# Two blocks or four at a time: the order of high and low matmuls in 128-feature tiles

## The chip, the cores and the metric

The kernel runs on one core of a Trainium2 chip. The metric is the device time of one execution in microseconds (us). The core has five engines that are meant here by these names: PE (TensorE, the matmuls), PEld (its weight loads), DVE (VectorE), ACT (ScalarE), POOL (GpSimd); SP (SyncE) issues the DMA transfers.

## What is computed

The reference is a two-layer decoder trunk over 256 tokens of width 2048. Cut to what matters for the matmuls:

```
u = rms_norm(x) @ w_in                      # 2048 x 2048, each layer
token_out = pooling mixer (layer 0) or differential attention (layer 1)
x = x + concat(token_out, mem_out) @ w_out  # 2048 x 2048, each layer
h = rms_norm(x)
z = relu(h @ w_ff1)                         # 2048 x 8192, each layer
x = x + (z * z) @ w_ff2                     # 8192 x 2048, each layer
```

There are also the key and value projections of a memory of 256 tokens and, between the layers, the shared keys and values. All inputs and outputs are fp32.

## The kernel before

**Two parts for each number.** Every fp32 weight and every fp32 activation is split into a high part (rounded to the matmul's fp32r format) and a low part (the rest). A product is the sum of three matmuls: high by high, high weight by low activation, low weight by high activation.

**The weights' way.** Weights are laid out in blocks of 128x128 in the order in which they are used, and eight blocks make one row in memory. The class `Feed` (lines 106 to 250) loads rows by SP, and splits them ahead of use: `_split` (lines 152 to 160) lets ACT cast 128x512 to the high ring (line 157) and lets DVE subtract to make the low ring (line 158). Four blocks that lie side by side in the rings, 512 columns, are called a quad here. Each ring has six slots of 512 columns. `fill`, called when a quad is begun, splits up to three jobs ahead of the one in use, if slots are free. ACT's cast into a slot waits for PE's last read of the high part there; DVE's subtraction waits for the cast and for PE's last read of the low part there.

**A tile of 128 features** is made by `a_part` (lines 377 to 397). A result has 128 features by 256 tokens. The weight block is the stationary operand, and the activations `xs[:, k, :]` are the moving one, with 256 columns of high parts and 256 of low parts next to each other. So the high block takes one matmul of 512 columns ("wide", line 391) into a whole bank of 512 columns, and the low block one matmul of 256 columns ("narrow", line 393) into the bank's second half, by the high activations alone. Both halves are added when the bank is emptied. `a_part` takes two blocks at a time: two wide matmuls, then two narrow ones, and again. A tile with 2048 inputs takes 16 blocks, four quads, and so eight such rounds.

```
            for c, k, hi, lo in two:
                nc.tensor.matmul(ps, hi, xs[:, k, :], start=first and c == 0, stop=False)
            for c, k, hi, lo in two:
                nc.tensor.matmul(
                    ps[:, T : 2 * T], lo, xs[:, k, 0:T], start=False,
                    stop=last and c == len(ks) - 1,
                )
```

Its callers: `group_u` (the pooling mixer's inputs, 12 tiles), `out_tiles` (w_out, 32 tiles), `up_tile` and `down_tile` of `ffn` (w_ff1 and half of w_ff2, 191 tiles). Together these are 235 tiles and 3760 blocks, a wide and a narrow matmul for each.

**Other matmuls from the rings.** `wide_step` (lines 412 to 421) makes the weights the moving operand: only wide matmuls, lines 417 to 419. `product` (lines 741 to 748) does the same for the other half of w_ff2. `c_tile` (lines 400 to 409) and `group_w` (lines 1020 to 1022) use narrow matmuls only, three for each block.

**In the feed-forward part** the bank of an up or down tile, `x_bank`, is a single one. After each tile ACT copies it out (`evict`, line 672), and `product` runs 6 or 9 wide matmuls on other banks before the next tile begins. In the last stretch of a feed-forward part, single `product` jobs stand between the quads of a tile.

**What sets the order.** The lines of the program give the order in which work is asked for; `at` and `tick` put small steps (attention, activation functions, splits) at the ends of quads. A scheduler then sets each engine's own queue; its order of ACT's and DVE's instructions follows the readiness that it expects, so that a change in PE's order can move them too.

Of the kernel before, what the change touches and what calls it, by code (L numbers as in the profile page):

```python
# [19 lines left out]
T = 256  # L20
NK = 16
# [241 lines left out]
def program(ctx, tc, plan, dry, xT, memT, par, lam, cst, wst, yT):  # L263
    nc = tc.nc
# [7 lines left out]
    feed = Feed(nc, wst, wp, tp, plan, dry)  # L272
# [10 lines left out]
    def tick():  # L283
        now[0] += 1
        for fn in pend.pop(now[0], []):
            fn()
# [9 lines left out]
    def mmt(name):  # L296
        return pp.tile([P, 512], F32, tag="mm", bufs=3, name=name)
# [79 lines left out]
    def a_part(ps, w, l, n, ks, xs, first=True, last=True, between=None):  # L377


        ks = list(ks)  # L380
        i = 0
        while i < len(ks):
            if between:
                between(i)
            two = []
            for k in ks[i : i + 2 - feed.pos % 2]:
                two.append((i, k % NK, *feed.block((w, l, k, n, 1))))
                feed.used()
                i += 1
            for c, k, hi, lo in two:  # L390
                nc.tensor.matmul(ps, hi, xs[:, k, :], start=first and c == 0, stop=False)  # L391
            for c, k, hi, lo in two:
                nc.tensor.matmul(  # L393
                    ps[:, T : 2 * T], lo, xs[:, k, 0:T], start=False,
                    stop=last and c == len(ks) - 1,
                )
            if feed.pos % 4 == 0:
                tick()

# [248 lines left out]
    def ffn(l, xs, tags, done):  # L648
# [57 lines left out]
        def up_tile(q, i, ps):  # L706
            a_part(ps, "w_ff1", l, q * NK + i, range(NK), xs)
            if not r:
                r.append(rstd_from("x"))
            y = evict(ps)  # L710

            def first():
                nc.vector.tensor_add(y[:, 0:T], y[:, 0:T], y[:, T : 2 * T])
                stt(y[:, 0:T], y[:, 0:T], 0.0, r[0], ALU.max, ALU.mult)

            at(1, first)
            at(3, lambda: nc.scalar.activation(stage[i % 8], y[:, 0:T], AF.Square))  # L717
            if q == 0 or i > 0:
                convert(i, 3)

        def down_tile(q, n, ps, between=None):
            end = l == 1 and q == 3 and n == 7
            if end:
                c_tile(ps, "w_ff2", l, n, range(q * NK, q * NK + NK), z)
                nc.vector.tensor_add(resid[:, n, :], resid[:, n, :], ps[:, 0:T])
                done(n)
                return
            a_part(ps, "w_ff2", l, n, range(q * NK, q * NK + NK), z, between=between)
            x = evict(ps)

            def add():
                nc.vector.tensor_add(resid[:, n, :], resid[:, n, :], x[:, 0:T])
                nc.vector.tensor_add(resid[:, n, :], resid[:, n, :], x[:, T : 2 * T])
                if q == 3:
                    done(n)

            at(1, add)
# [152 lines left out]
    xs = sp.tile([P, NK, 512], F32R, tag="S2", name="xs0")  # L890
# [67 lines left out]
    ps = [mmt("mq0"), pp.tile([P, 512], F32, tag="o", bufs=1, name="mq0")]  # L958
# [22 lines left out]
    def group_u(g):  # L981
        up = ups[g % 2]
        for c in range(3):
            ps = mmt("u")
            a_part(ps, "w_in", 0, 3 * g + c, range(NK), xs)
            low = vt("u_c")
            nc.scalar.copy(low, ps[:, T : 2 * T])
            nc.vector.tensor_add(low, ps[:, 0:T], low)
            nc.vector.tensor_mul(up[:, c, 16:], low, x_r[0])
# [106 lines left out]
    def pair_of_banks(c, name):  # L1096
        if c % 2:
            return [pp.tile([P, 512], F32, tag="s", bufs=2, name=name) for _ in range(2)]
        return [mmt(name) for _ in range(2)]
# [3 lines left out]
    for c in range(3):  # L1103
        ps = pair_of_banks(c, "k1")
# [10 lines left out]
    for c in range(3):  # L1115
        ps = pair_of_banks(c + 1, "v1")
# [9 lines left out]
    ps = pair_of_banks(0, "mk1")  # L1126
# [4 lines left out]
    ps = pair_of_banks(1, "mv1")  # L1131
# [132 lines left out]
    for c in range(3):  # L1264
        ps = pair_of_banks(0, "q1")
# [14 lines left out]
    for h in range(4):  # L1280
        ps = mmt("mq1")
# [95 lines left out]
```

## Time and profile before

| what | value |
|---|---|
| median of 3 runs | 2045.59 us (2045.58 to 2047.15) |
| the profiled execution | 2044.93 us |
| its span, first to last instruction | 2043.1 us |
| granted TensorE clock | 1.00 |
| wide matmuls of line 391 | 3760, mean recorded length 395 to 401 ns |
| narrow matmuls of line 393 | 3760, mean recorded length 278 to 281 ns |
| weight loads | 11060, one for each matmul, most of them 188 ns |
| DMA, mean over the span | 191 GB/s |

Recorded lengths of matmuls overlap: a matmul begins before the one ahead of it has ended. What a matmul costs PE is therefore read from the distance between two starts, which the timeline gives, and not from its length. "Idle before" is the time that an engine stood still ahead of an instruction, with the one that ended it.

### The profile page before, as it was taken

What the parts mean: (1) busy time and instruction counts of PE and PEld (TensorE: products, weight loads), DVE (VectorE), ACT (ScalarE), POOL (GpSimd) and SP (SyncE); (2) the same over time, 40 slices, a digit from 0 to 9 for tenths busy, and PEclk for the clock granted to TensorE, in tenths of its full rate; (3) what the DMA queues carried; (4) which work ended last, traced back from release to release, by engine and by line L of the source; (5) the groups of instructions that cost most, each with busy time, mean ns of one, the idle gap of its engine ahead of it and who ended that gap; (6) DMA issues with size and microseconds to landing.
All of it is one profiled execution on the core that took longest, in us unless ns stands there. A gap on an engine that the chain in (4) does not pass through costs nothing.

```text
span 2043.1 us, 32257 instructions
## 1 busy us (share of the span) xinstructions
PE 2037.2 (100%) x11060; PEld 1755.3 (86%) x11060; DVE 1716.2 (84%) x3215; ACT 1349.8 (66%) x2505; POOL 51.9 (3%) x67
## 2 busy tenths in 40 slices
PE   9999999999999999999999999999999999999999
PEld 8888888888888888888888888888888888888888
DVE  8888889889879978999766687889879978988997
ACT  7765566666666756768665697566657666666764
POOL 0001200000000000000000000310000000000000
PEclk9999999999999999999999999999999999999999
DMA  9556556555555555655565543656555555565564
GB/s 314 178 181 190 188 174 206 197 196 197 186 201 202 189 207 191 207 169 182 194 228 186 170 140 103 196 166 207 196 196 205 186 196 196 186 210 195 196 209 135
DMA packets 110470, 390.75 MB, mean 191 GB/s; under 512 B 12256, under 2 KB 14944, under 8 KB 110304
## 3 DMA queue, kind: packets, MB, share of 16 engines
q1 hardware_dynamic: 110160, 388.59, 57.1%
q8 instruction: 86, 1.41, 0.3%
q14 instruction: 80, 0.66, 0.1%
q10 hardware_dynamic: 144, 0.10, 0.0%
HBM read 386.54 MB, written 2.10 MB: 190 GB/s over the span
## 4 chain that ended last, share of the span: by engine, by line
PE 99%; ACT 1%; DVE 1%; issue 0%
PE x_bank L391 33%; PE x_bank L393 16%; PE wo L391 6%; PE p L746 5%; PE p L747 5%; PE p L748 5%; PE wo L393 3%; PE u L391 2%; PE ff L391 2%; PE u L393 1%; PE k L417 1%; PE k L419 1%; PE v L417 1%; PE k L418 1%; PE v L419 1%; PE v L418 1%
## 5 line engine op out<-in xcount | busy, mean ns | idle before, releaser
L157 ACT CAST hi_ring<-raw 128x512 fp32r<-128x512 f32 x1193 | 736.7, 620 | 529.5 <-PE x_bank L391 308.0
L158 DVE TENSOR_TENSOR lo_ring<-raw,hi_ring 128x512 fp32r<-128x512 f32 x1193 | 817.2, 695 | 206.7 <-ACT hi_ring L157 165.5
L391 PE MATMUL x_bank<-fx,hi_ring 128*128 128x512 f32 x1920 | 602.1, 395 | 0.0
L393 PEld LDWEIGHTS x_bank<-fx,lo_ring 128*128 128x128 f32 x1920 | 361.0, 188 | 83.6
L393 PE MATMUL x_bank<-fx,lo_ring 128*128 128x256 f32 x1920 | 377.4, 278 | 0.0
L391 PEld LDWEIGHTS x_bank<-fx,hi_ring 128*128 128x128 f32 x1920 | 301.4, 189 | 9.3
L391 PE MATMUL x_bank<-z,hi_ring 128*128 128x512 f32 x960 | 301.1, 395 | 0.0
L158 DVE TENSOR_TENSOR lo_ring<-slab,hi_ring 128x1024 fp32r<-128x1024 f32 x188 | 230.1, 1224 | 54.3 <-ACT hi_ring L157 53.6
L157 ACT CAST hi_ring<-slab 128x1024 fp32r<-128x1024 f32 x188 | 196.9, 1047 | 73.1 <-PE x_bank L391 36.2
L393 PEld LDWEIGHTS x_bank<-z,lo_ring 128*128 128x128 f32 x960 | 180.5, 188 | 41.7
L393 PE MATMUL x_bank<-z,lo_ring 128*128 128x256 f32 x960 | 188.8, 278 | 0.0
L391 PE MATMUL wo<-cat,hi_ring 128*128 128x512 f32 x512 | 162.5, 398 | 0.5 <-DVE resid L639 0.5
L391 PEld LDWEIGHTS x_bank<-z,hi_ring 128*128 128x128 f32 x960 | 151.9, 189 | 6.5 <-ACT room L672 0.4
L393 PEld LDWEIGHTS wo<-cat,lo_ring 128*128 128x128 f32 x512 | 95.9, 188 | 21.7
L672 ACT COPY room<-x_bank 128x512 f32<-128x512 f32 x180 | 104.9, 583 | 2.0 <-PE x_bank L393 2.0
L393 PE MATMUL wo<-cat,lo_ring 128*128 128x256 f32 x512 | 101.4, 279 | 0.0
L746 PE MATMUL p<-hi_ring,sit 128*128 128x512 f32 x256 | 100.5, 393 | 0.0
L747 PE MATMUL p<-hi_ring,sit 128*128 128x512 f32 x256 | 100.2, 391 | 0.0
L748 PE MATMUL p<-lo_ring,sit 128*128 128x512 f32 x256 | 99.7, 389 | 0.0
L391 PEld LDWEIGHTS wo<-cat,hi_ring 128*128 128x128 f32 x512 | 79.1, 189 | 2.2 <-PE wo L393 0.9
L717 ACT ACTIVATE room<-room 128x256 f32<-128x256 f32 x128 | 53.2, 416 | 39.1 <-DVE room L300 39.1
L746 PE MATMUL p<-hi_ring,z 128*128 128x512 f32 x192 | 75.2, 392 | 0.0
(313 smaller groups left out, 3102.3 us busy)
## 6 DMA issues: line engine op xcount, KB each, us to landing
raw<-in_w SPq DMA_DIRECT2D x595, 512.0 KB, 4.0
slab<-in_w SPq DMA_DIRECT2D x124, 512.0 KB, 3.3
resid<-in_x SPq DMA_DIRECT2D x8, 256.0 KB, 5.9
room<-in_w SPq DMA_DIRECT2D x4, 512.0 KB, 4.2
memraw<-in_mem SPq DMA_DIRECT2D x4, 512.0 KB, 3.6
out_y<-resid SPq DMA_DIRECT2D x16, 128.0 KB, 1.8
memraw<-in_mem SPq DMA_DIRECT2D x7, 256.0 KB, 6.3
raw<-in_w SPq DMA_DIRECT2D x3, 256.0 KB, 3.5
```

Source lines behind the costliest of these rows:

```text
L157: self.nc.scalar.copy(hi, src)
L158: self.nc.vector.tensor_sub(lo, src, hi.bitcast(F32))
L391: nc.tensor.matmul(ps, hi, xs[:, k, :], start=first and c == 0, stop=False)
L393: nc.tensor.matmul(ps[:, T : 2 * T], lo, xs[:, k, 0:T], start=False, stop=last and c == len(ks) - 1,)
L417: nc.tensor.matmul(ps[t], xl, hi, start=k == 0, stop=False)
L418: nc.tensor.matmul(ps[t], xh, hi, start=False, stop=False)
L419: nc.tensor.matmul(ps[t], xh, lo, start=False, stop=k == NK - 1)
L672: nc.scalar.copy(x, ps)
L717: at(3, lambda: nc.scalar.activation(stage[i % 8], y[:, 0:T], AF.Square))
L746: nc.tensor.matmul(ps, a[1], hi, start=first, stop=False)
L747: nc.tensor.matmul(ps, a[0], hi, start=False, stop=False)
L748: nc.tensor.matmul(ps, a[0], lo, start=False, stop=last)
```

## The change

`a_part` takes all blocks of a quad at once (four, or as many as are left of it), and does the wide matmuls of the high parts together and the narrow ones of the low parts together. A group that begins at block 4 or 12 of its tile does its low parts first. A tile of 16 blocks so runs 4 wide, 8 narrow, 8 wide, 8 narrow, 4 wide, where it ran 2 wide, 2 narrow eight times over. The numbers of matmuls and weight loads, their operands and the sums are the same; the ends of quads (`tick`, `between`) stay where they were. Lines after `a_part` are moved down by two.

```diff
-            two = []
-            for k in ks[i : i + 2 - feed.pos % 2]:
-                two.append((i, k % NK, *feed.block((w, l, k, n, 1))))
+            some = []
+            for k in ks[i : i + 4 - feed.pos % 4]:
+                some.append((i, k % NK, *feed.block((w, l, k, n, 1))))
                 feed.used()
                 i += 1
-            for c, k, hi, lo in two:
-                nc.tensor.matmul(ps, hi, xs[:, k, :], start=first and c == 0, stop=False)
-            for c, k, hi, lo in two:
-                nc.tensor.matmul(
-                    ps[:, T : 2 * T], lo, xs[:, k, 0:T], start=False,
-                    stop=last and c == len(ks) - 1,
-                )
+            end = last and i == len(ks)
+            low_first = some[0][0] % 8 == 4
+            for low in (low_first, not low_first):
+                for c, k, hi, lo in some:
+                    stop = end and low != low_first and c == len(ks) - 1
+                    if low:
+                        nc.tensor.matmul(ps[:, T : 2 * T], lo, xs[:, k, 0:T], start=False, stop=stop)
+                    else:
+                        nc.tensor.matmul(ps, hi, xs[:, k, :], start=first and c == 0, stop=stop)
             if feed.pos % 4 == 0:
                 tick()
```

## The prediction

> **What bounds the kernel now.** I read the page first: the busy shares, then the chain that ended last.
>
> ```profile
> PE 2037.2 (100%) x11060; PEld 1755.3 (86%) x11060; DVE 1716.2 (84%) x3215; ACT 1349.8 (66%) x2505; POOL 51.9 (3%) x67
> ...
> PE 99%; ACT 1%; DVE 1%; issue 0%
> PE x_bank L391 33%; PE x_bank L393 16%; PE wo L391 6%; PE p L746 5%; PE p L747 5%; PE p L748 5%; PE wo L393 3%; PE u L391 2%; PE ff L391 2%; PE u L393 1%; PE k L417 1%; PE k L419 1%; PE v L417 1%; PE k L418 1%; PE v L419 1%; PE v L418 1%
> ```
>
> PE is never free, and the chain is PE's own queue. Lines 391 and 393, which the change reorders, hold over 60% of it. The view of waits, for PE's weight loads, says whether PE ever stands still for data:
>
> ```profile
> PEld mt L592 <- DVE att L586: 1.2, 2, 1.0
> ...
> PEld x_bank L391 <- ACT room L672: 0.4, 2, 0.2
> ...
> PEld mk L419 <- DVE lo_ring L158: 0.2, 1, 0.2
> ```
>
> The total, the count and the longest wait stand behind each name. Weights from the rings cost a single wait of 0.2 us in the whole span. So only the distance between matmul starts can gain anything. The timeline of PE has it, first in the present order:
>
> ```profile
> 601.06 0.40 PE L393 MATMUL x_bank<-fx,lo_ring 128*128 128x256 f32 x2
> 601.29 0.63 PE L391 MATMUL x_bank<-fx,hi_ring 128*128 128x512 f32 x2
> 601.76 0.39 PE L393 MATMUL x_bank<-fx,lo_ring 128*128 128x256 f32 x2
> 601.99 0.63 PE L391 MATMUL x_bank<-fx,hi_ring 128*128 128x512 f32 x2
> 602.45 0.40 PE L393 MATMUL x_bank<-fx,lo_ring 128*128 128x256 f32 x2
> ```
>
> Two wide matmuls take 0.46 to 0.47 us, two narrow ones 0.23. A narrow run in `c_tile`, after a wide matmul:
>
> ```profile
> 1206.12 0.39 PE L419 MATMUL q<-lo_ring,x_mx 128*128 128x512 f32 x1
> 1206.35 0.28 PE L405 MATMUL mq<-x_mx,hi_ring 128*128 128x256 f32 x1
> 1206.46 0.28 PE L406 MATMUL mq<-x_mx,hi_ring 128*128 128x256 f32 x1
> 1206.58 0.28 PE L407 MATMUL mq<-x_mx,lo_ring 128*128 128x256 f32 x1
> ...
> 1207.18 0.28 PE L406 MATMUL mq<-x_mx,hi_ring 128*128 128x256 f32 x1
> 1207.30 0.28 PE L407 MATMUL mq<-x_mx,lo_ring 128*128 128x256 f32 x1
> ```
>
> From 1206.35 to 1207.30 are eight narrow steps in 0.95 us, 119 ns each, against 115.5 in the present pairs. The timeline rounds to 10 ns, so I took the starts of all matmuls from the trace and grouped them by runs of equal width (mean ns of a run, from its first start to the start behind it):
>
> | run | count | ns | |
> |---|---|---|---|
> | 2 wide between narrow | 1642 | 466.7 | |
> | 2 narrow between wide | 1847 | 231.0 | |
> | 8 wide between narrow | 128 | 1825.1 | 8 x 227.0 + 9.1 |
> | 11 wide between narrow | 56 | 2503.2 | 11 x 227.0 + 6.2 |
> | 372 wide (`wide_step`) | 1 | 84440 | 227.0 each |
> | first 8 narrow of a long run behind a wide one | 5 | 937, 937, 952, 953, 958 | mean 947.4 |
>
> So a wide matmul costs 227.0 in a long run and a narrow one 119 to 120. A wide run after narrow ones costs 6 to 13 ns on top; the first two narrow ones after a wide one are 8 to 9 ns cheaper together. A round of two and two takes 697.7 ns against 2 x 227.0 + 2 x 119.5 = 693: alternating costs some 4.7 ns a round.
>
> **The change: fewer rounds.** Nothing is removed: 3760 wide and 3760 narrow matmuls stay. In the feed-forward parts (180 tiles on `x_bank`) a tile stands between `product` runs of m wide matmuls, and its outer wide matmuls join these.
>
> - Before: eight narrow pairs, seven inner wide pairs, and a run of m + 2: 8 x 231.0 + 7 x 466.7 + 227.0(m + 2) + 9.1 = 5578.0 + 227.0m.
> - After: two narrow runs of eight, a wide run of eight, a run of m + 8: 2 x 947.4 + 1825.1 + 227.0(m + 8) + 9.1 = 5545.0 + 227.0m.
> - Gain 33.0 ns, times 180: 5.9 us.
>
> The other 55 tiles mostly follow one another: 8 x 697.7 = 5581.6 before, 2 x (1825.1 + 947.4) = 5545.0 after, 36.6 each, 2.0 us. Together 7.9 us. Of the 470 narrow runs of eight that this counts, the built order of the changed kernel has 436; the rest are cut by jobs between quads, by transposes, or begin off the quad. 7.9 x 436 / 470 = **7.4 us**.
>
> The unknown is the narrow run of eight low blocks; no such run is in the trace. The rows for it are narrow runs whose weights are the same block twice, then a low one. The end rows 937 and 958 move the sum by 436 x 10.5 ns, 4.6 us each way: gains of 2.8 to 12.0 us. I take the mean, since the five rows spread evenly about it.
>
> **What moves with it, at no cost.** Three waits had to be looked at.
>
> - *Low parts sooner.* In a quad that does low first, the low blocks are needed 2 x 233 = 466 ns sooner than now. Pairing the n-th subtraction of line 158 with the n-th job on PE, the low parts of an `a_part` quad are ready 4.46 us (median) before use, 3.03 at the lowest twentieth, 0.97 at the least.
> - *High slots free later.* There the last high read begins at the quad's last step instead of before the last two narrow ones, 231 ns later; ACT's cast into that slot, DVE's subtraction behind it and all that is queued behind both can be that much later. Both together take 697 ns; the least lead of 0.97 us still covers it. In quads with the high parts first, slots come free sooner.
> - *The eviction.* `x_bank` is a single bank. Now ACT's copy (L672) is queued behind a cast that waits for the last wide matmul of the same tile; it ends 292 ns (median; 90 at the least) before the bank's next matmul, whose weight load begins up to 227 ns before that: the cover is thin. In the built order of the changed kernel the last matmul of a tile is wide, begins 227 ns before the tile's end instead of 117, and should release ACT 430 ns after its start, as L747 at 607.76 releases the cast at 608.19: 0.2 us behind the end. The casts queued ahead of the copy all wait for matmuls at least twelve earlier. The copy so begins some 0.2 us behind the tile's end where it now begins 0.5 us behind it (549.83 against 549.29). If ACT were late there instead, 180 tiles would pay what it is late by.
>
> The scheduler also shifts DVE's and ACT's order and a few DMA issues by one place; DVE is busy 84%, ACT 66%, and DMA brings 191 GB/s with loads three rows ahead, so none of it is late. PE's waits on ACT rise from 931 to 1103, those on DVE stay (1420, 1417); the 2351 waits of now cost PE and PEld some 11 us in all, nearly none of it on the rings, so I count none.
>
> The profiled execution (2044.93 us, span 2043.1) would go to 2037.5. The median of runs is 0.66 above it: 2045.59 - 7.4 = **2038.2 us**.
>
> **Rivals.**
>
> 1. *The order is free.* Each step depends on its own width alone, and the 4.7 ns a round are an artefact of the recorded starts: 0 to 2 us gained, 2045.6. For it: the excess is 0.7% of a round and the narrow pairs give most of it back. Against it: 1642 rounds agree to a few ns. [...]
>
> 2. *Long narrow runs are bound by weight loads*, which ends slower. A load is recorded as 188 ns, a narrow step is 115 to 120, so loads overlap; eight different blocks in a row have never been asked of them, only pairs. The longest repeated step in the narrow rows is 125. At 115 + 7 x 125 = 990 ns a run, 436 x 42.6 ns = 18.6 us are lost against my sum: 11.2 slower, 2056.8. It decides from 964 ns a run (120.6 a step); at 188 a step the loss would pass 200 us. Against it: runs of 28 narrow steps hold 119 to 121, and a third of their loads are new blocks. The Trainium skill (TensorE: Matmul & The Clock Gate, LDWEIGHTS) gives 128 / 1.2 = 107 ns for a load, an estimate by its figure; by it this rival falls away.
>
> 3. *Weights come late.* If the new order costs one cast (620 ns) more of lead than the 697, only the three quads with leads of 0.97 to 1.25 us wait, 0.5 us in all: the gain is 6.9, 2038.7.
>
> 4. *It does not do what it says*: the scheduler could cut the runs. The built order speaks against it (narrow pairs between wide ones fall from 1847 to 5); if transposes make the cut runs dearer, 2 to 4 us of gain are left, 2042.6.
>
> **How the numbers follow.** The forecast has 0.70 (rival 3 within it), rival 1 0.14, rival 2 0.08, rival 4 0.07, and a late eviction 0.01. About 4 us, 0.2%, is what a measurement of this kernel can tell from no change. Of the forecast, narrow runs over 955 ns gain less than that: I put 0.08 of its 0.70 there. Faster: 0.70 - 0.08 = 0.62. Same: 0.08 + 0.14 + 0.07 = 0.29. Slower: 0.08 + 0.01 = 0.09. The range goes from the lowest narrow row (2045.6 - 12.0 = 2033.6) up to 2045.0, which takes in rival 4 and the upper part of the rows, and half of rival 1.
>
> **What would show it.** In the changed profile: wide runs of eight at 1825 ns and their inner steps at 227; narrow runs of eight at 937 to 958; no wait of PE on lo_ring or hi_ring above 1 us in total; the copy of `x_bank` starting 0.2 us after its tile; line 398's total distance falling more than that of 396 rises. Narrow runs over 964, or `x_bank` loads waiting on ACT room, would make the prediction wrong.

## The result and the profile after

The changed kernel takes 2049.52 us (median of 17 runs, 2048.96 to 2051.55) against 2045.58 (17 runs, 2044.97 to 2047.15): ratio 1.002, 95% interval 1.0012 to 1.0027. It is 3.9 us slower; 7.4 us faster was forecast. The page of its profiled execution (2051.55 us, the longest of the 17), the lines that answer to those shown of before:

```profile
span 2049.8 us, 32161 instructions
...
PE 2043.1 (100%) x11060; PEld 1767.3 (86%) x11060; DVE 1721.1 (84%) x3215; ACT 1350.2 (66%) x2505; POOL 61.5 (3%) x67
...
PE 98%; ACT 1%; DVE 1%; DMA 0%; issue 0%; DVEq 0%
PE x_bank L398 32%; PE x_bank L396 17%; PE wo L398 6%; PE p L748 5%; PE p L749 5%; PE p L750 5%; PE wo L396 3%; PE u L398 2%; PE ff L398 2%; PE u L396 1%; PE ff L396 1%; PE q L419 1%; PE q L420 1%; PE q L421 1%; PE k L419 1%; PE k L420 1%
```

PE still bounds everything, and its share is the same. The busy sum of matmuls says nothing here, since recorded lengths overlap. The timeline of PE shows the new runs, each row being one run with its start:

```profile
552.35 1.07 PE L398 MATMUL x_bank<-z,hi_ring 128*128 128x512 f32 x4
553.25 1.12 PE L396 MATMUL x_bank<-z,lo_ring 128*128 128x256 f32 x8
554.21 2.00 PE L398 MATMUL x_bank<-z,hi_ring 128*128 128x512 f32 x8
556.05 1.12 PE L396 MATMUL x_bank<-z,lo_ring 128*128 128x256 f32 x8
557.00 1.09 PE L398 MATMUL x_bank<-z,hi_ring 128*128 128x512 f32 x4
557.93 0.39 PE L748 MATMUL p<-hi_ring,z 128*128 128x512 f32 x1
```

From start to start, eight narrow steps take 0.95 to 0.96 us, as expected; the eight wide ones from 554.21 to 556.05 take 1.84, where 1.825 was expected. From all starts in the trace, as in the prediction (mean ns of a run):

| run in the changed kernel | count | expected | measured |
|---|---|---|---|
| 8 narrow between wide | 436 | 947.4 (937 to 958) | 952.5 |
| 8 wide between narrow | 244 | 1825.1 | 1840.9 |
| 14 wide (product and tile) | 128 | 3187.1 | 3200.9 |
| 17 wide (product and tile) | 56 | 3865.2 | 3880.8 |

The steps inside such runs (median ns each) show where it goes:

```
wide behind 2 narrow, before              233 231 227 227 227 227 227 227
wide behind 8 narrow, after               233 236 228 232 231 227 227 227
wide_step run behind transposes, before   316 231 231 236 228 232 231 227
narrow behind wide, after                 113 119 120 120 120 120 120 120
```

A wide run settles to 227 ns in two steps behind a narrow pair, at 10 ns in all, and in five behind eight narrow matmuls, at 25. The third row, a run at 1195.51 us in the trace of before, has the same slow settling after its first step.

Where the loss lies, between the first matmuls of stages (us, profiled executions):

| stretch | before | after | difference |
|---|---|---|---|
| feed-forward, layer 0, `x_bank` tiles | 652.77 | 653.85 | +1.08 |
| feed-forward, layer 1, `x_bank` tiles | 652.74 | 653.82 | +1.08 |
| mixer, first tiles of feed-forward, w_out of layer 0 | 227.45 | 228.04 | +0.59 |
| w_out of layer 1 | 98.30 | 101.03 | +2.73 |
| all else (most of it code that is untouched) | 408.36 | 409.53 | +1.17 |

The third row adds up four stretches (before: 86.23, 93.00, and 24.11 for the first tiles of either layer). With the last row the profiled execution is 6.65 us longer from the warm-up to the last matmul, though the medians differ by 3.9. So two things had to be explained: steps that cost more instead of less, and a stretch of 98 us that got 2.7 us longer. Of these 2.7 us, 1.6 belong to this one execution: the granted clock fell to 0.50 there for 3.4 us, as the experiment on w_out shows.

### The profile page after: what moved, and what is told of

Same layout as the page of the kernel before. It is cut to its first block, busy times and chain, and to the rows that moved or that the text cites. A ratio compares the mean times of both kernels' runs of the same rounds, so it can differ in the third digit from the quotient of the medians.

```text
span 2049.8 us, 32161 instructions
## 1 busy us (share of the span) xinstructions
PE 2043.1 (100%) x11060; PEld 1767.3 (86%) x11060; DVE 1721.1 (84%) x3215; ACT 1350.2 (66%) x2505; POOL 61.5 (3%) x67
## 4 chain that ended last, share of the span: by engine, by line
PE 98%; ACT 1%; DVE 1%; DMA 0%; issue 0%; DVEq 0%
PE x_bank L398 32%; PE x_bank L396 17%; PE wo L398 6%; PE p L748 5%; PE p L749 5%; PE p L750 5%; PE wo L396 3%; PE u L398 2%; PE ff L398 2%; PE u L396 1%; PE ff L396 1%; PE q L419 1%; PE q L420 1%; PE q L421 1%; PE k L419 1%; PE k L420 1%
## 5 line engine op out<-in xcount | busy, mean ns | idle before, releaser
L398 PE MATMUL x_bank<-fx,hi_ring 128*128 128x512 f32 x1920 | 499.8, 392 | 0.0
L398 PEld LDWEIGHTS x_bank<-fx,hi_ring 128*128 128x128 f32 x1920 | 345.3, 189 | 60.3
L396 PEld LDWEIGHTS x_bank<-fx,lo_ring 128*128 128x128 f32 x1920 | 261.9, 190 | 18.7
L396 PE MATMUL x_bank<-fx,lo_ring 128*128 128x256 f32 x1920 | 267.7, 282 | 0.0
L398 PE MATMUL x_bank<-z,hi_ring 128*128 128x512 f32 x960 | 251.4, 392 | 0.0
L396 PEld LDWEIGHTS x_bank<-z,lo_ring 128*128 128x128 f32 x960 | 132.1, 190 | 10.0
L396 PE MATMUL x_bank<-z,lo_ring 128*128 128x256 f32 x960 | 135.1, 282 | 0.0
L398 PE MATMUL wo<-cat,hi_ring 128*128 128x512 f32 x512 | 133.3, 397 | 0.6 <-DVE cat L300 0.4
L715 DVE TENSOR_TENSOR room<-room 128x256 f32<-128x256 f32 x128 | 54.3, 424 | 57.0 <-ACT room L674 56.8
L396 PE MATMUL wo<-cat,lo_ring 128*128 128x256 f32 x512 | 74.8, 284 | 0.0
```

What stands on the lines that cost most here:

```text
L396: nc.tensor.matmul(ps[:, T : 2 * T], lo, xs[:, k, 0:T], start=False, stop=stop)
```

## The experiments

Theory N: a wide run starts dear or cheap by what ran before it, and behind four or more narrow matmuls it costs some 15 ns more than behind two. Rival R is the prediction's own reading, that each alternation costs the same. Rival E is that the low-first quads and the wide tile ends cost. For the stretch of w_out: theory W, PE waits for attention results; rival S, it is chance.

**Four blocks, always high first** (`low_first = False` in the changed kernel):

```diff
-            low_first = some[0][0] % 8 == 4
+            low_first = False
```

> Four blocks at a time as in the changed kernel, but every quad does its high parts first: runs of 4 wide and 4 narrow, 940 rounds, tiles end narrow. Theory N (a wide run costs 22 to 25 ns on top when four or more narrow matmuls ran before it, 9 to 13 when two did): a quad takes 930 + 473 = 1403 ns against 1395 of before, a feed-forward tile 36 ns more, another tile 31 ns more; 180 x 36.5 + 55 x 31 = +8.3 us, 2053.9, slower also than the changed kernel. Theory R (as predicted: each alternation costs the same 4.7 ns): 917 + 471 a quad, -6 us, 2039. Theory E (the low-first quads and wide tile ends are what costs): wide runs of four at 917, at or below before.

Measured 2057.64 us, ratio 1.0061 (1.0048 to 1.0075): 11.9 slower than before, though it alternates half as often. The timeline of PE:

```profile
561.23 1.08 PE L398 MATMUL x_bank<-z,hi_ring 128*128 128x512 f32 x4
562.15 0.64 PE L396 MATMUL x_bank<-z,lo_ring 128*128 128x256 f32 x4
562.62 1.09 PE L398 MATMUL x_bank<-z,hi_ring 128*128 128x512 f32 x4
563.55 0.63 PE L396 MATMUL x_bank<-z,lo_ring 128*128 128x256 f32 x4
564.02 1.09 PE L398 MATMUL x_bank<-z,hi_ring 128*128 128x512 f32 x4
```

From 561.23 to 562.62 a quad takes 1.39 us, from 562.62 to 564.02 it takes 1.40: over the trace 929.5 + 473.4 = 1402.9 ns, as N has it. R is refuted, by sign and by 18 us. The loss is larger than N's 8.3, since the `product` runs that now begin behind four narrow matmuls settle still longer: a run of ten takes 2312 ns, 42 over 10 x 227. Its steps are 235, 233, 236, 224, 231, 236, 228, 232, 231 and then 227 ns (medians): nine steps, where a run behind eight narrow matmuls settles in five.

**Two blocks, in turn high first and low first:**

```diff
-            for k in ks[i : i + 4 - feed.pos % 4]:
+            for k in ks[i : i + 2 - feed.pos % 2]:
...
-            low_first = some[0][0] % 8 == 4
+            low_first = some[0][0] % 4 == 2
```

> Two blocks at a time, in turn high first and low first: again runs of 4 wide and 4 narrow, but half of the groups begin with low parts and tiles end wide. Theory N: the same steps as with four blocks high first, +8 us, 2054. Theory R: -6 us. Theory E: slower than four blocks high first, since it has twice the low-first groups of the changed kernel.

Measured 2058.93 us, ratio 1.0067 (1.0054 to 1.0079). The runs cost what they did in the last kernel (wide fours 930.2, narrow fours 473.1), though half of the groups are low first and tiles end wide. So it is the lengths of the runs, not E; the 1.3 us between the two are within the intervals, and the `x_bank` tiles of layer 0 take 657.96 us in the one and 657.95 in the other.

**One block, in turn high first and low first:**

```diff
-            for k in ks[i : i + 4 - feed.pos % 4]:
+            for k in ks[i : i + 1]:
...
-            low_first = some[0][0] % 8 == 4
+            low_first = some[0][0] % 2 == 1
```

> One block at a time, in turn high first and low first: runs of 2 wide and 2 narrow as before, but half of the blocks low first, and tiles end wide. Theory N: steps as before (466.7 and 231.0 a round), within 1 us of before apart from waits that a moved ACT or DVE step may cost. Theory R: the same number of rounds as before, so the same. Theory E: slower than before by 2 us or more.

Measured 2044.62 us, ratio 0.9995 (0.9987 to 1.0004): no difference from before. The wide end of a tile joins the `product` run:

```profile
562.17 0.63 PE L398 MATMUL x_bank<-z,hi_ring 128*128 128x512 f32 x2
562.64 0.39 PE L396 MATMUL x_bank<-z,lo_ring 128*128 128x256 f32 x2
562.87 0.40 PE L398 MATMUL x_bank<-z,hi_ring 128*128 128x512 f32 x1
563.10 0.39 PE L748 MATMUL p<-hi_ring,sit 128*128 128x512 f32 x1
```

Pairs cost 466.8 and 230.6, as before. With as many low-first groups as high-first ones and every tile ending wide, E is refuted a second time.

**Narrow runs of one to eight** (a single run; j low parts ahead of the four high ones in each second quad):

```diff
+            ahead = 0
+            if some[0][0] % 8 == 4:
+                ahead = turn_no[0] % 5
+            todo = [(1, x) for x in some[:ahead]] + [(0, x) for x in some] + [(1, x) for x in some[ahead:]]
...
```

(`turn_no` counts the tiles; the matmuls follow the order of `todo`.)

> A measurement in the trace, not a contender: in the second quad of each pair j low parts run ahead of the four high ones, j = 0 to 4 by the tile's number, so that wide runs of four stand behind narrow runs of 1 to 8. Theory N: a wide run of four takes 917 to 921 ns behind one or two narrow, and 928 to 933 behind four to eight; three lies between or at the upper value. A debt that goes on growing with each narrow matmul would show 925 behind four and over 945 behind eight. Theory R: 917 behind any.

Its one time was 2053.56 us. Wide runs of four took, behind 1, 2, 3, 4, 5, 6 and 7 narrow matmuls, 922, 923, 917, 930, 930, 930 and 930 ns (medians), and a run of eight behind 8 took 1841, over 8 x 227 by 25. So the first four steps cost the same from four narrow matmuls on, and no debt grows with their number. Theory N missed below four: 922 and 923 are over its 921, and three gave 917, where it had more. It is not the narrow run alone that decides there: behind 2 that stand behind four wide, a wide run takes 15 over, behind 2 in the long rows of before 6 to 9. Runs of ten, which begin with `product` matmuls, took 34, 37, 7 and 43 ns over 10 x 227 behind 1, 2, 3 and 4 narrow ones (medians).

**w_out of layer 1 alone, and all but it:**

```diff
+            size = 4 if (w, l) == ("w_out", 1) else 2
-            for k in ks[i : i + 4 - feed.pos % 4]:
+            for k in ks[i : i + size - feed.pos % size]:
...
-            low_first = some[0][0] % 8 == 4
+            low_first = size == 4 and some[0][0] % 8 == 4
```

(`!=` in place of `==` for the second kernel.)

> The change for the 16 tiles of w_out in layer 1 alone; all other tiles take two blocks at a time as before. Theory W (part of the loss is PE waiting in these tiles for attention results, which the wide matmuls of a whole quad want sooner): 2 to 2.7 us over before, 2048, and the stretch from the first wo to the first ff of layer 1 2 to 3 us longer than 98.3. Rival S (the loss is matmul steps everywhere, and what the trace shows there is chance): 16 of 235 tiles, 0.3 us, the same as before.

> The change for all tiles but the 16 of w_out in layer 1. Theory W: what the matmul steps cost alone, 180 x 10 to 12 ns in the feed-forward parts and 0.5 us elsewhere: 1.5 to 2.5 us over before, 2047.6; the stretch from the first wo to the first ff of layer 1 stays at 98.3. Rival S: as the changed kernel, 3.9 us over before.

Measured: alone 2047.06 us, ratio 1.001 (1.0001 to 1.0019); all but it 2048.38, ratio 1.0015 (1.0006 to 1.0024), against 2045.36 of before. The stretch takes 99.43 us in the first and 98.27 in the second, 98.30 in before. The view of waits for this stretch, the first kernel:

```profile
PEld mt L595 <- DVE att L589: 1.8, 1, 1.8
PE mt L595 <- DVE att L589: 1.3, 1, 1.3
...
PEld wo L399 <- DVE cat L300: 1.1, 2, 0.8
```

and the second, where the change is left out there:

```profile
PEld mt L595 <- DVE att L589: 1.2, 2, 0.9
```

PE waits for the last heads of the memory attention (`mt`, line 592 of before) and for the splits of `cat`, the moving operand of w_out. The rest of the 2.73 us is no wait. The order on PE is the same in this stretch for the first of these kernels and the changed one; here are four wide matmuls and then four narrow ones of it, first in the changed kernel:

```profile
1267.08 2.27 PE L398 MATMUL wo<-cat,hi_ring 128*128 128x512 f32 x4
1269.14 1.04 PE L396 MATMUL wo<-cat,lo_ring 128*128 128x256 f32 x4
```

and then with the change in w_out of layer 1 alone:

```profile
1264.18 1.28 PE L399 MATMUL wo<-cat,hi_ring 128*128 128x512 f32 x4
1265.30 0.63 PE L397 MATMUL wo<-cat,lo_ring 128*128 128x256 f32 x4
```

From start to start, the four wide ones take 2.06 us in the changed kernel and 1.12 in the other. The view of stretches gives the granted clock of the changed kernel's profiled execution there, as the third figure from the end:

```profile
1266.62:1270.03 3.41, 3.41 (x12) 2.84 (x12) 1.72 (x11) 1.64 (x8) 0.00 (x0) 0.50 0.00 0
```

It is 0.50 for these 3.41 us and 1.00 in the rest of the stretch; in the other kernel it is 1.00 throughout. The matmuls in this time take 1.59 of the 1.60 us that lie between 101.03 and 99.43; what made the clock fall is not shown. Without it both executions put the cost of the change in this stretch at 1.1 us.

W holds in direction: the change costs time in this stretch only where it is made there. Its size is 1.1 us, under the 2 to 3 expected, and the medians are too wide to tell (alone 1.7, 0.2 to 3.9 by the interval; all but it 3.0, where W had 1.5 to 2.5 and S 3.9). Its reason, that the wide matmuls of a whole quad come sooner, is not enough: four blocks high first do the same, and there the stretch takes 98.84 us, 0.5 over before, which 16 tiles at 31 ns of dearer steps account for. Whether it is the low-first order, the eight wide matmuls in a row or the places of ACT's and DVE's instructions was not tried. The steps alone account for 1.07 + 1.08 us in the feed-forward parts of the second kernel, the same as in the changed one to 0.01 us.

**Eight blocks at a time**, one long narrow run a tile (frees of ring slots moved behind the group's matmuls):

```diff
+            wide = not between and len(ks) == 16 and (w, l) != ("w_out", 1) and start % 4 == 0
+            size = (8, 8)[g % 2] if wide else 2 - feed.pos % 2
+            g += 1
...
+            low_first = wide and g % 2 == 0
...
+            for q in ends:
+                feed.done(q)
+                tick()
```

> Eight blocks at a time, in turn high first and low first, in tiles of 16 blocks that begin at a quad's start, but not in w_out of layer 1, which stays as before, nor where jobs stand between quads: 8 wide, 16 narrow, 8 wide. One long wide run and one long narrow run per tile. Theory N (a wide run starts 22 to 25 ns dearer, 42 at worst, however long the narrow run before it; a narrow run begins 8 ns cheaper and goes on at 120 a step): 1912 + 227 x (16 + m) + 25 = 5569 + 227m a tile against 5578 + 227m of before: 1.5 to 2.2 us faster than before, 2043.5; at 42 it would be 2 us slower. The ring of six slots holds the tile's two or more quads longer: if weights then come late, the waits on hi_ring and lo_ring show it, and the time is over 2050.

Measured 2047.66 us, ratio 1.0011 (1.0002 to 1.002). The timeline has the runs wanted:

```profile
561.00 2.08 PE L413 MATMUL x_bank<-z,lo_ring 128*128 128x256 f32 x16
562.91 2.00 PE L415 MATMUL x_bank<-z,hi_ring 128*128 128x512 f32 x8
564.75 0.39 PE L766 MATMUL p<-hi_ring,sit 128*128 128x512 f32 x1
```

Sixteen narrow steps take 1912.4 ns and the wide run of 22 behind them 5014 (median, 20 over): a tile with m = 6 takes 6927 ns against 6933 of before (medians of whole tiles), 6 less where N has 9. But the mean of that wide run is 5042 in layer 0 and 5030 in layer 1, for a wait that the view of waits names:

```profile
PEld x_bank L415 <- ACT room L692: 4.6, 19, 0.8
```

The bank's eviction comes late 19 times: 28 and 16 ns a run are 2.4 us over 112 runs, more than the 6 ns a tile that the runs give. A version without these waits was not tried.

**Three, three and two blocks**, high first (`size = (3, 3, 2)[g % 3]`, `low_first` always false, else as the last kernel):

> Three, three and two blocks at a time, high first always, in the same tiles as low16. Wide runs of three behind three narrow ones: in the run with varied narrow lengths a wide run behind three started 9 ns dear, against 15 behind two. Theory N in its measured form: 691 + 354 + 691 + 354 + 464 + 231 = 2785 ns for eight blocks against 2791, 11 ns a tile, 2.3 us faster than before: 2043.3. If the start of a wide run hangs on more than the narrow run just before it, wide threes take up to 698 and the gain is gone.

Measured 2049.31 us, ratio 1.002 (1.001 to 1.0029): slower. Wide threes behind three narrow take 696.8 ns, the upper value, and wide threes behind two 697.1. The 9 ns seen behind three narrow in the kernel of varied lengths were those of another history (the three stood behind four wide matmuls, and those behind five narrow ones). What a wide run costs at its start is known for repeated runs of one length, and not as a function of the last narrow run alone.

Per round of n wide and n narrow, over n x (227 + 120) ns: 3.7 for n = 2 (697.7), 9.3 for 3 (696.8 + 353.5), 14.9 for 4, 17.4 for 8 (1840.9 + 952.5), 14 for 16.

## Why the prediction was wrong

The step that failed is the one that reads "A wide run after narrow ones costs 6 to 13 ns on top", and with it 1825.1 + 9.1 in the sum of a tile. The rows of 8 and 11 wide all stand behind narrow pairs. I carried them over to wide runs behind eight narrow matmuls, without saying that no such run is in the trace; for the narrow run I said so and put a range on it. Measured: 15.8 ns more for 244 runs of eight, 13.8 for 128 of fourteen, 15.6 for 56 of seventeen, 6.5 us together. The runs behind transposes, in the trace of before, would have warned: the one shown settles in six steps after its first, 27 ns in all.

Point by point:

- *PE bounds, and only steps can gain*: right for what PE does; the tile of before was computed as 6940 ns for m = 6, and its pairs in the feed-forward parts make it 6936.
- *The narrow run of eight*: 952.5, inside 937 to 958, 5 ns over the value taken, 2.2 us. With the 6.5 the forecast of -7.4 becomes +1.3; counted by tiles it is +11 ns x 180 = +2.0, and the two feed-forward stretches show 2.2. With the 0.6 of the third row of the table and the 1.1 of w_out in layer 1 this makes 3.9, the difference of the medians.
- *Alternating costs some 4.7 ns a round*: not a constant. Over steps of 227 and 120 ns a round of two costs 3.7 and one of eight 17.4, where the sum took 1825.1 + 947.4, 3.5 below such steps. To gain, one round in the place of four had to cost under 3.7 x 4 = 14.8.
- *Weights sooner, slots later, at no cost*: right. The waits of PE and PEld name lo_ring and hi_ring for 0.4 and 0.3 us in the changed kernel.
- *The eviction*: right to the number. It begins 199 ns behind the tile's end (496 before) and ends 578 ns (292) before the bank's next matmul. The row of ACT, whose copy starts 0.20 us behind the 557.93 shown above:

```profile
558.13 0.59 ACT L674 COPY room<-x_bank 128x512 f32<-128x512 f32 x1 [1.26 <-PE x_bank L398]
```

- *What was not looked at*: the moving operand. In w_out of layer 1 the activations come just in time, and PE waits longer for them in the new order: 1.1 us. Which part of the new order does it stays open.
- *Rival 1* (order is free) came nearest in time, for a wrong reason: order moves this kernel by up to 13 us. The Trainium skill (TensorE: Matmul & The Clock Gate, Back-to-back issue gap) gives the isolated gap of a matmul by its own width alone, N / 2.4 + 2.5 ns, and says that in a stream of loads and matmuls both set the spacing. Width alone does not give the spacing here: the same eight matmuls take 1402.9 ns in fours, high first, and 1395.4 in pairs.
- *Rival 2* (narrow runs bound by loads) gave the sign, not the cause: narrow steps stay at 120, sixteen in a row. *Rival 3*: none of the reordered matmuls waited for the rings. *Rival 4*: the runs are as the diff says, 436 of eight.

What stays open: why a wide run needs five steps to settle behind eight narrow ones and nine behind four, and what it is that outlasts a run; what in w_out of layer 1 makes PE wait; what made the clock fall; and the 1.2 us in the last row of the table, 0.6 of it in the opening one (to the first `mq`), whose main part lies between 44.07 and 45.84 us over the profiled executions of these kernels.

## What to carry to other kernels

A cost per alternation, read from one run length, does not hold for another: before summing, ask of each run in the new order whether the trace has one with the same run before it, and give a range to those that it has not. Where PE is never idle, regrouping matmuls of two widths moved single steps here by up to 9 ns, and pairs were already as good as anything tried here. When matmuls are brought forward, check both operands: the one that streams can come just in time as well. And before a longer stretch of one profiled execution is put down to a change, look at its granted clock.

## What was not expected of the hardware

A wide run settles by what ran before it, and repeatably. These are its steps in ns (medians), each row ending where 227 is reached:

```
behind narrow pairs, before, 8 wide                       233 231 227
behind 8 narrow, changed kernel                           233 236 228 232 231 227
behind 16 narrow, eight blocks at a time                  233 236 228 233 231 227
behind 1 narrow, varied lengths, 13 wide                  231 224 231 236 228 232 231 227
behind 4 narrow, four blocks high first, 10 wide          235 233 236 224 231 236 228 232 231 227
```

Apart from its first step, and to 1 ns, each row is the end of the last one. It reads as one sequence, which a run enters earlier or later by what ran before it; why is not shown. More than the last run counts: in the feed-forward parts of before the wide pairs take 469 and 463.5 ns in turn, and the narrow ones 232.4 and 228.4, though every round is alike in the program.

A plain fp32 matmul of 256 columns (line 1197 of before) begins 216 ns behind the one ahead of it, one of 128 columns (line 1226) 109 ns. The rings' fp32r matmuls, of twice the columns, take 227 and 120.
